# Expert weights in rows of 16 KB, and down into one bank: a transformer pair on one Trainium2 core

## The chip, the cores and the metric

One core of a Trainium2 chip runs the whole program; the other cores have no part in it. The metric is the device time of one execution in microseconds (us). The kernel before took 2298.34 us (median of 3 runs, 2297.22 to 2298.34). A difference of 0.2%, some 4.6 us, is about the least that can be told from no change.

## The reference, cut to what matters

Two blocks follow each other on 256 tokens of width 1024, all in float32. The first block has a modulation from a vector `c` (`w_ada`, 1024 by 6144), projections (`w_in`, 1024 by 3072) with retention and dilated attention, an output product, and a mixture of 16 experts. The second block is two rounds of FFN, gated recurrent mixer, FFN.

```
mod = silu(c) @ w_ada + b_ada                   # six parts of 1024
h = rmsnorm(x, g_pre_mix) * (1 + scale_m) + shift_m
proj = h @ w_in                                 # retention q, k, v, gate; attention q, k, v
x = x + gate_m * rmsnorm(mixed @ w_out, g_post_mix)
h = rmsnorm(x, g_pre_ffn) * (1 + scale_f) + shift_f
affinity = softmax(h @ w_router)                # 256 x 16
gates, idx = top_k(affinity.T, 32)              # each expert takes its 32 best tokens
for e in range(16):
    xe = h[idx[e]]                              # 32 x 1024
    ye = (silu(xe @ w_gate[e]) * (xe @ w_up[e])) @ w_down[e]   # 1024 -> 2048 -> 1024
    out[idx[e]] += ye * gates[e]
x = x + gate_f * rmsnorm(out, g_post_ffn)
```

The three weights of an expert are 8 MiB each, 24 MiB together; 16 experts are 384 MiB, each byte read once.

## The kernel before, in words

The kernel is written in a tile framework: a scheduler orders the instructions of each engine beforehand, by priorities and estimated times, and sets the waits; `s.queue` pins an instruction behind another of its engine. Each engine then works its list in that order. All large loads are issued by SP, in order, and a load waits at the head of SP's list until its buffer is free.

**Units.** `unit` (L53) loads a weight block of 8 KB a partition (1 MiB) into a ring. The first block has two rings, `ring` with RA = 4 and `ringb` with RB = 7 buffers, taken in a fixed mixture: 11 MiB ahead at most. The second block has `ring` alone.

**The front.** `mod_bank` (L226) forms part i of the modulation by products with 32 equal columns, a unit being two tiles of 128 rows; the later parts are summed on VectorE, a unit at a time (`mod_unit`, L278, called by `mod_step`). The projections take `w_in` in units of 256 columns, so that a row of a unit is 1 KB (`unit(c)`, L383). `pieces` (L253) splits them in high and low parts on ScalarE, VectorE and GpSimd; `chan` (L385) makes one tile of 128 channels from a unit. Sixteen such tiles follow each other (L574), and between them the modulation and the attention and retention heads. `shift` (L424) reads units 6, 8, 10 and 11 once more.

**Routing.** The affinities are sorted, and one-hot matrices `sall` of token against slot are made. `gather0(k)` (L727) picks the first expert's rows of tile k of the model width, `gathers(k)` (L730) those of all 16 experts, each by four products.

**Experts** (`experts`, L793). For each expert, and each k of 8 tiles of the model width, a unit of gate and one of up: 128 rows of 2048 columns, so that a row of a unit is 8 KB and a partition holds one row. Each unit serves four products of 32 stationary columns against 512 moving ones (L817), the four groups of FFN columns standing in four groups of 32 rows of one PSUM bank. For the first expert `gather0` and `gathers` stand between the units, and the last six of its units that find no place in the ring (`more`, L767) go to tiles that serve no more. Then silu, product, transposes to `ht` (L835), and down: units of two groups of 128 rows of 1024 columns, so that a row is 4 KB; eight products a unit (L855) into two banks `dn`, one for each half of the model width, four row groups in each. `fin` adds the result of an expert to the tokens during the next. The last expert takes down by columns, 512, 256 and 256 (L875), in rows of 2 KB and 1 KB, so that what stands behind the last weights is small: one copy `pr` (L885) of 256 columns, products with the gates (L887), and `rms` (L324).

**Second block.** `boundary` (L958) normalises, and FFN's first units are already being loaded: two units (gate and up half of its first 256 columns) stand in SP's list behind the last expert's.

## Time and profile before

| | us |
|---|---|
| median of three runs | 2298.34 |
| profiled execution, its span | 2296.9 |
| what lies around the span (median less span) | 1.4 |
| front, until the first product of an expert | 192.6 |
| experts, until the last weights of down are used | 192.6 to 1133.1 |
| second block, from its first FFN product | 1148.9 to 2296.9 |

The page gives one profiled execution. Its first part is busy time by engine; its second cuts the span in 40 slices of 57.4 us and shows the share of each engine in tenths, the granted clock of TensorE, the share of the 16 DMA engines and the GB/s that they moved. The chain is followed back from the last instruction to whatever released each step. PE is TensorE, PEld its weight loads, DVE VectorE, ACT ScalarE, POOL GpSimd, SP the queue that issues loads. A float32 product is shown as two instructions.

### The profile page before, as it was taken

What the parts mean: (1) busy time and instruction counts of PE and PEld (TensorE: products, weight loads), DVE (VectorE), ACT (ScalarE), POOL (GpSimd) and SP (SyncE); (2) the same over time, 40 slices, a digit from 0 to 9 for tenths busy, and PEclk for the clock granted to TensorE, in tenths of its full rate; (3) what the DMA queues carried; (4) which work ended last, traced back from release to release, by engine and by line L of the source; (5) the groups of instructions that cost most, each with busy time, mean ns of one, the idle gap of its engine ahead of it and who ended that gap; (6) DMA issues with size and microseconds to landing.
All of it is one profiled execution on the core that took longest, in us unless ns stands there. A gap on an engine that the chain in (4) does not pass through costs nothing.

```text
span 2296.9 us, 30296 instructions
## 1 busy us (share of the span) xinstructions
PE 1989.6 (87%) x12509; PEld 1334.1 (58%) x12509; DVE 987.9 (43%) x1582; ACT 739.2 (32%) x1224; POOL 155.8 (7%) x164
## 2 busy tenths in 40 slices
PE   7898877777777776767599999999999999999998
PEld 5684211111111111111199999899999998989997
DVE  7984100000000010000275568965556556896554
ACT  4552000000000000000154456845445444684443
POOL 1321000000000000000100032200000003200000
PEclk8997887777888788888799999999999999999999
DMA  8978999999999999999975545546556564544651
GB/s 307 367 292 310 413 417 417 416 417 417 416 417 417 418 417 417 417 417 417 342 247 190 196 158 183 175 149 236 183 174 205 181 207 152 192 165 160 226 180 60
DMA packets 258264, 659.64 MB, mean 287 GB/s; under 512 B 12371, under 2 KB 166219, under 8 KB 225742
## 3 DMA queue, kind: packets, MB, share of 16 engines
q1 hardware_dynamic: 256396, 657.08, 75.9%
q8 instruction: 98, 1.61, 0.3%
q10 hardware_dynamic: 1730, 0.64, 0.1%
q14 instruction: 40, 0.33, 0.0%
HBM read 656.62 MB, written 1.05 MB: 286 GB/s over the span
## 4 chain that ended last, share of the span: by engine, by line
PE 51%; DMA 38%; DVE 4%; POOL 2%; ACT 1%; issue 1%; POOLq 0%; SPq 0%; DVEq 0%; ACTq 0%
DMA w<-in_w_up_e_dram 22%; DMA w<-in_w_down_e_dram 12%; PE up L96 8%; PE up L98 8%; PE up L97 8%; PE acc L98 6%; PE acc L97 6%; PE acc L96 6%; PE up L131 3%; DMA w<-in_w_gate_e_dram 3%; PE up L135 2%; PE acc L817 2%; POOL uc L1187 1%; DVE macc L286 1%; DVE v L1218 1%
## 5 line engine op out<-in xcount | busy, mean ns | idle before, releaser
L83 DVE TENSOR_TENSOR hl<-w,hl 128x1024 fp32r<-128x1024 f32 x376 | 457.5, 1229 | 253.8 <-ACT hl L82 253.8
L82 ACT ACTIVATE hl<-w 128x1024 fp32r<-128x1024 f32 x388 | 404.8, 1057 | 271.1 <-PE up L98 105.3
L96 PE MATMUL up<-hTh,hl 128*128 128x256 f32 x1664 | 470.1, 283 | 1.2 <-ACT uc L1208 1.2
L97 PE MATMUL up<-hTl,hl 128*128 128x256 f32 x1664 | 467.4, 281 | 0.0
L98 PE MATMUL up<-hTh,hl 128*128 128x256 f32 x1664 | 467.4, 281 | 0.0
L96 PEld LDWEIGHTS up<-hTh,hl 128*128 128x128 f32 x1664 | 313.3, 188 | 4.0 <-ACT uc L1208 1.9
L97 PEld LDWEIGHTS up<-hTl,hl 128*128 128x128 f32 x1664 | 313.6, 188 | 2.0
L98 PEld LDWEIGHTS up<-hTh,hl 128*128 128x128 f32 x1664 | 313.5, 188 | 0.0
L855 PE MATMUL up<-w,tmp 128*32 128x512 f32 (+1 forms) x1048 | 222.0, 629 | 55.9 <-DMA w<-in_w_down_e_dram 51.5
L832 DVE TENSOR_TENSOR tmp<-tmp,acc 128x512 f32<-128x512 f32 x16 | 11.0, 687 | 498.8 <-PE acc L817 498.8
L96 PE MATMUL acc<-hl,a 128*128 128x512 f32 x528 | 209.9, 397 | 0.0
L97 PE MATMUL acc<-hl,a 128*128 128x512 f32 x528 | 208.6, 395 | 0.0
L98 PE MATMUL acc<-hl,e 128*128 128x512 f32 x528 | 208.5, 395 | 0.0
L821 ACT ACTIVATE tmp<-acc 128x512 f32<-128x512 f32 x16 | 9.6, 597 | 580.8 <-PE acc L817 580.8
L855 PEld LDWEIGHTS up<-w,tmp 128*32 128x32 f32 x1048 | 48.9, 114 | 217.7 <-DMA w<-in_w_down_e_dram 130.9
L817 PE MATMUL acc<-w,rqk 128*32 128x512 f32 x480 | 97.1, 896 | 51.8 <-DMA w<-in_w_up_e_dram 26.3
L817 PE MATMUL acc<-w,ak 128*32 128x512 f32 x480 | 92.5, 860 | 56.9 <-DMA w<-in_w_gate_e_dram 30.0
L817 PE MATMUL acc<-w,rv 128*32 128x512 f32 x480 | 97.3, 898 | 49.9 <-DMA w<-in_w_gate_e_dram 25.0
L147 POOL TENSOR_TENSOR y<-v,mhalf 128x1 f32<-128x1 f32 x22 | 12.2, 554 | 1827.8 <-DVE v L143 1819.9
L871 DVE COPY pr<-up 128x512 f32<-128x512 f32 x15 | 10.4, 692 | 248.5 <-PE up L855 248.5
L98 PEld LDWEIGHTS acc<-hl,e 128*128 128x128 f32 x528 | 99.0, 187 | 24.3 <-DVE e L916 0.2
L96 PEld LDWEIGHTS acc<-hl,a 128*128 128x128 f32 x528 | 99.1, 188 | 21.4
(371 smaller groups left out, 2364.6 us busy)
## 6 DMA issues: line engine op xcount, KB each, us to landing
w<-in_w_gate_e_dram SPq DMA_DIRECT2D x126, 1024.0 KB, 19.8
w<-in_w_up_e_dram SPq DMA_DIRECT2D x125, 1024.0 KB, 19.8
w<-in_w_down_e_dram SPq DMA_DIRECT2D x123, 1024.0 KB, 17.9
w<-in_ffn_w_up_dram SPq DMA_DIRECT2D x88, 1024.0 KB, 5.3
w<-in_w_in_dram SPq DMA_DIRECT2D x52, 1024.0 KB, 6.6
w<-in_ffn_w_down_dram SPq DMA_DIRECT2D x44, 1024.0 KB, 5.7
w<-in_w_ada_dram SPq DMA_DIRECT2D x24, 1024.0 KB, 9.0
w<-in_w_out_dram SPq DMA_DIRECT2D x12, 1024.0 KB
```

What stands on the lines that cost most here:

```text
L82: a = s.nc.scalar.activation(t[:, 0], src, AF.Copy)
L83: b = (eng or s.nc.vector).tensor_tensor(t[:, 1], src, t[:, 0].bitcast(F32), OP.subtract)
L96: a = mm(out, st[0], mv[0], start=start, stop=False)
L97: mm(out, st[0], mv[1], start=False, stop=False)
L98: s.mm = mm(out, st[1], mv[0], start=False, stop=stop)
L131: a = mm(out, h[0][:, k, tok(t)], ws[k // 4][i][:, k % 4, :], start=k + i == 0, stop=False)
L135: s.mm = mm(out, h[1][:, k, tok(t)], ws[k // 4][0][:, k % 4, :], start=False, stop=k == KT - 1)
L286: s.nc.vector.scalar_tensor_tensor(acc, w[:, a, :], c, acc, OP.mult, OP.add)
L817: T.matmul(gu[i][32 * g:32 * g + 32, :], xk, u[g], start=k == 0, stop=k == KT - 1)
L855: T.matmul(dn[n][32 * g:32 * g + 32, c], ht[:, j, 32 * g:32 * g + 32], u(g), start=j == 0, stop=j == 3)
L1187: G.tensor_tensor(nx[:, lo:], cur[:, lo:], cur[:, lo - sh:16 + S - sh], OP.add)
L1218: V.scalar_tensor_tensor(v, c[:, 13 + k:13 + k + S], self.cw[:, k, hd:hd + 1], v, OP.mult, OP.add)
```

## The change

- **Blocks** (`block`, new): 2 MiB, 16 KB a partition. Two blocks of three go to `ringb` (now 4 buffers of 16 KB) by one load, each third goes to two buffers of `ring` by two loads of 8 KB rows at a pitch of 16 KB. So 12 MiB ahead at most, six blocks. All large weights of the first block go through `block`.
- **Gate and up**: a block is 256 rows of the weight, partition p holding rows 2p and 2p + 1 one behind the other: 16 KB in a row. To match, the tiles of the model width are woven: tile k of x, of the one-hot gathers, of the router weights and of the two factors `af` and `bf` takes every second channel of a group of 256 (`pairs`; `fcol` has the bias and gain columns in that order).
- **Down**: a block is 512 rows, partition p holding rows 4p to 4p + 3: 16 KB in a row. The transposes of h take every fourth column (`hj`). The eight products of a row set go to one bank `dn`: half n of the width in rows 64n to 64n + 63, odd and even j in the two groups of 32 of it. One copy `pr` of 512 columns follows instead of two, and the products with the gates take 64 rows for each half.
- **Last expert**: down is taken as for the others; the three column parts are gone.
- **First expert**: `gathers` of all eight tiles stand behind the transposes of h, ahead of the gates' transposes and of down, and no longer between the units. Four `gather0` stand ahead of the first product, not two. The last 6 MiB of its first weights go to the same idle tiles as before, as three blocks.
- **Projections**: `w_in` in blocks of 512 columns (rows of 2 KB), each used by four tiles; the attention values take 512 moving columns in two banks. `w_ada` comes as blocks of four tiles of 128 rows, `w_out` likewise.
- A reserve for dynamic DMA descriptors is made smaller in the constructor; comments are dropped.

```diff
-RA, RB = 4, 7
+RA, RB = 4, 4
...
-        r = s.ring
-        if s.ringb is not None and s.nunit * RB % (RA + RB) < RB:
-            r = s.ringb
         if t is None:
-            s.nunit += 1
-            t = r.tile([P, 2048], F32, tag="w", name="w")
+            t = s.ring.tile([P, 2048], F32, tag="w", name="w")
...
+    def block(s, view):
+        s.nblock += 1
+        sh = view.shape
+        if s.nblock % 3 == 0:
+            h = sh[1] // 2
+            return [s.unit(view[:, i * h:(i + 1) * h]) for i in range(2)]
+        t = s.ringb.tile([P, 4096], F32, tag="w", name="w")
+        if len(sh) == 3:
+            t = t.rearrange("p (a b) -> p a b", a=sh[1])
+        s.udma = s.nc.sync.dma_start(t, view)
+        h = sh[1] // 2
+        return [t[:, :h], t[:, h:]]
...
+    def ada(s, I, i, u):
+        return s.block(I["w_ada"][0, u * 512:(u + 1) * 512, i * D:(i + 1) * D].rearrange("(a p) n -> p a n", p=P))
     def mod_bank(s, I, i):
         pt = s.bank("up")
-        for u in range(4):
-            w = s.unit(I["w_ada"][0, u * 256:(u + 1) * 256, i * D:(i + 1) * D].rearrange("(a p) n -> p a n", p=P))
-            for a in range(2):
+        for u in range(2):
+            w = s.ada(I, i, u)
+            for a in range(4):
                 for n in range(2):
-                    r = 32 * (2 * a + n)
-                    s.nc.tensor.matmul(pt[r:r + 32, :], s.cb[:, 2 * u + a, :], w[:, a, half(n)], start=u == 0, stop=u == 3)
+                    r = 32 * (2 * (a % 2) + n)
+                    k = 4 * u + a
+                    s.nc.tensor.matmul(pt[r:r + 32, :], s.cb[:, k, :], w[a // 2][:, a % 2, half(n)], start=k < 2, stop=k > 5)
...
-    def mod_unit(s, I, i, u, acc, first):
-        w = s.unit(I["w_ada"][0, u * 256:(u + 1) * 256, i * D:(i + 1) * D].rearrange("(a p) n -> p a n", p=P))
+    def mod_unit(s, w, u, acc, first):
...
+    def pairs(s, ap, k):
+        return ap.rearrange("p (q c r) -> p q r c", r=2, c=P)[:, k // 2, k % 2, :]
...
+        wide = lambda c: s.block(wv[:, :, c * 512:(c + 1) * 512])
+        us = {}
+        def chan(c, j, n):
             pt = s.bank("up")[:, :n]
-            for q, w in enumerate(s.pieces(u[:, :, tok(j)])):
+            if c // 2 not in us:
+                us[c // 2] = wide(c // 2)
+            o = (c % 2) * S + j * P
+            for q in range(2):
+                w, = s.pieces(us[c // 2][q][:, :, o:o + P])
...
-        us = {c: unit(c) for c in (10, 11, 6, 8)}
-        for q, c in enumerate((10, 11)):
-            pt = s.bank("up", (2, S))
-            ws = s.pieces(us[c])
-            for t in range(2):
-                for k in range(KT):
-                    w = ws[k // 2]
-                    s.mm3(pt[:, t, :], (h[0][:, k, tok(t)], h[1][:, k, tok(t)]), (w[0][:, k % 2, :], w[1][:, k % 2, :]), k == 0, k == KT - 1)
-            A.activation(av[:, :, q * S:(q + 1) * S], pt, AF.Copy)
+        us = {c: wide(c) for c in (5, 3, 4)}
+        pts = [s.bank("up") for t in range(2)]
+        for q in range(2):
+            for i, w in enumerate(s.pieces(us[5][q])):
+                k = 4 * q + i
+                for t in range(2):
+                    s.mm3(pts[t], (h[0][:, k, tok(t)], h[1][:, k, tok(t)]), (w[0][:, 0, :], w[1][:, 0, :]), k == 0, k == KT - 1)
+        for t in range(2):
+            A.activation(av[:, t, :], pts[t], AF.Copy)
...
-            s.mod_unit(I, j, u, accm[j], j > 2)
+            if u % 2 == 0:
+                accm["w"] = s.ada(I, j, u // 2)
+            s.mod_unit(accm["w"][u % 2], u, accm[j], j > 2)
...
-        wu = {c: wo(c) for c in (2, 3, 0, 1)}
+        wu = {}
+        for c in (1, 0):
+            wu[2 * c], wu[2 * c + 1] = s.block(I["w_out"][0, c * 512:(c + 1) * 512, :].rearrange("(j p) n -> p j n", p=P))
...
-                T.matmul(pt, xh[:, t, tok(k)], sl, start=t == 0, stop=False)
-                T.matmul(pt, xl[:, t, tok(k)], sl, start=False, stop=t == 1)
+                T.matmul(pt, s.pairs(xh[:, t, :], k), sl, start=t == 0, stop=False)
+                T.matmul(pt, s.pairs(xl[:, t, :], k), sl, start=False, stop=t == 1)
...
-        more = [extra((pe, "dk", 2048, 1)), extra((pe, "yg", 2048, 1)), extra(wt, wt), extra(wt, wt),
-                extra((pa, "ya", 1024, 1), xt), extra(xt, tt, tt)]
+        more = [extra((pe, "dk", 2048, 1), (pe, "yg", 2048, 1)), extra(wt, wt, wt, wt),
+                extra((pa, "ya", 1024, 1), xt, xt, tt, tt)]
...
+        def load(w, e, r, x=None):
+            v = I[w][0, e, r[0]:r[1], :].rearrange("(p r) f -> p (r f)", p=P)
+            if x:
+                return x(v)
+            return [u[:, g * 512:(g + 1) * 512] for u in s.block(v) for g in range(4)]
...
+            for q in range(4):
                 if e == 0:
-                    for i in range(k + (k > 0), min(k + 2, KT)):
-                        gather0(i)
-                    if k:
-                        gathers(k - 1)
-                xk = xe[k // 2][:, k % 2, ec] if e else x0[:, k, :]
+                    for k in range(2 * q + (q > 0) * 2, min(2 * q + 4, KT)):
+                        gather0(k)
                 for i, w in enumerate(("w_gate_e", "w_up_e")):
-                    n = 2 * k + i - RA - RB
-                    v = I[w][0, e, tok(k), :]
-                    if e == 0 and n >= 0:
-                        u = more[n](v)
-                    else:
-                        u = s.unit(v)
-                        u = [u[:, g * 512:(g + 1) * 512] for g in range(4)]
-                    for g in range(4):
-                        T.matmul(gu[i][32 * g:32 * g + 32, :], xk, u[g], start=k == 0, stop=k == KT - 1)
-            if e == 0:
-                gathers(KT - 1)
+                    u = load(w, e, (256 * q, 256 * q + 256), more[i] if e == 0 and q == 3 else None)
+                    for r in range(2):
+                        k = 2 * q + r
+                        xk = xe[k // 2][:, k % 2, ec] if e else x0[:, k, :]
+                        for g in range(4):
+                            T.matmul(gu[i][32 * g:32 * g + 32, :], xk, u[4 * r + g], start=k == 0, stop=k == KT - 1)
...
+            hj = h.rearrange("p (c j) -> p j c", j=4)
             for j in range(4):
-                T.transpose(pt[:, j, :], h[:, tok(j)], s.ident)
+                T.transpose(pt[:, j, :], hj[:, j, :], s.ident)
             ht = s.tmp().rearrange("p (j c) -> p j c", j=4)
             A.activation(ht, pt, AF.Copy)
+            if e == 0:
+                for k in range(KT):
+                    gathers(k)
...
+                for t in range(2):
+                    for n in range(2):
+                        T.matmul(py[t][n], s.ident, ye[t][:, half(n)], start=True, stop=False)
...
-            dn = [s.bank("up") for _ in range(2)]
-            wd = I["w_down_e"][0, e].rearrange("(g j p) n -> p j g n", g=4, p=P)
-            def down(n, j, u, c=slice(0, 512)):
-                for g in range(4):
-                    T.matmul(dn[n][32 * g:32 * g + 32, c], ht[:, j, 32 * g:32 * g + 32], u(g), start=j == 0, stop=j == 3)
-            pr = pa.tile([P, D], F32, tag="xn", name="pr", bufs=2)
-            if e < NE - 1:
+            dn = s.bank("up")
+            for g in range(4):
+                u = load("w_down_e", e, (512 * g, 512 * g + 512), more[2] if e + g == 0 else None)
                 for j in range(4):
-                    us = []
-                    for q in range(2):
-                        v = wd[:, j, 2 * q:2 * q + 2, :]
-                        if e + j + q == 0:
-                            us += more[-1](v)
-                        else:
-                            u = s.unit(v)
-                            us += [u[:, a, half(n)] for a in range(2) for n in range(2)]
                     for n in range(2):
-                        down(n, j, lambda g: us[2 * g + n])
-                A.activation(pr[:, half(0)], dn[0], AF.Copy)
-                V.tensor_copy(pr[:, half(1)], dn[1])
-            else:
+                        r = 64 * n + 32 * (j % 2)
+                        T.matmul(dn[r:r + 32, :], ht[:, j, 32 * g:32 * g + 32], u[2 * j + n], start=g == 0 and j < 2, stop=g == 3 and j > 1)
+            pr = pa.tile([P, 512], F32, tag="xn", name="pr", bufs=2)
+            V.tensor_copy(pr, dn)
+            if e == NE - 1:
                 res = [([], py[t]) for t in range(2)]
-                for n, c in ((0, slice(0, 512)), (1, slice(0, 256)), (1, slice(256, 512))):
-                    w = c.stop - c.start
-                    o = slice(n * 512 + c.start, n * 512 + c.stop)
-                    m = 512 // w
-                    for t in range(2):
-                        T.matmul(py[t][n][:, c], s.ident, ye[t][:, o], start=True, stop=False)
-                    for j in range(0, 4, m):
-                        u = s.unit(wd[:, j:j + m, :, o])
-                        for i in range(m):
-                            down(n, j + i, lambda g: u[:, i, g, :], c)
-                    V.tensor_copy(pr[:, o], dn[n][:, c])
-                    for t in range(2):
-                        T.matmul(py[t][n][:, c], gT[:, tok(t)], pr[:, o], start=False, stop=True)
-                        res[t][0].append((py[t][n][:, c], o))
+                for t in range(2):
+                    for n in range(2):
+                        r = slice(64 * n, 64 * n + 64)
+                        T.matmul(py[t][n], gT[r, tok(t)], pr[r, :], start=False, stop=True)
+                        res[t][0].append((py[t][n], half(n)))
             def fin(t, e=e, gT=gT, pr=pr):
                 for n in range(2):
                     pt = s.bank("tr")
-                    T.matmul(pt, gT[:, tok(t)], pr[:, half(n)], start=True, stop=True)
+                    r = slice(64 * n, 64 * n + 64)
...
+                    T.matmul(pt, gT[r, tok(t)], pr[r, :], start=True, stop=True)
```

## Rows read from the trace of the kernel before

**Rows 1.** The page: DMA share and GB/s in 40 slices, and the packets

```profile
DMA  8978999999999999999975545546556564544651
GB/s 307 367 292 310 413 417 417 416 417 417 416 417 417 418 417 417 417 417 417 342 247 190 196 158 183 175 149 236 183 174 205 181 207 152 192 165 160 226 180 60
DMA packets 258264, 659.64 MB, mean 287 GB/s; under 512 B 12371, under 2 KB 166219, under 8 KB 225742
```

**Rows 2.** The chain in order of time: start us, us, what

```profile
242.43 19.85 DMA w<-in_w_up_e_dram
...
324.13 18.80 DMA w<-in_w_down_e_dram
...
1048.38 18.47 DMA w<-in_w_down_e_dram
```

**Rows 3.** Windows: PE, PEld, DVE, ACT, POOL busy, clock, DMA share, GB/s; two experts, whole stage

```profile
324.00:340.00 16.00, 11.85 (x58) 2.90 (x54) 1.05 (x3) 0.87 (x2) 0.00 (x0) 1.00 1.03 409
344.00:380.00 36.00, 23.91 (x126) 3.69 (x120) 3.45 (x5) 0.60 (x1) 0.00 (x0) 0.83 1.01 421
1048.00:1064.00 16.00, 11.82 (x58) 2.73 (x54) 1.05 (x3) 1.47 (x3) 0.00 (x0) 0.92 1.03 409
1068.00:1104.00 36.00, 27.76 (x128) 4.65 (x124) 3.44 (x5) 0.60 (x1) 0.00 (x0) 0.78 1.02 422
264.00:1108.00 844.00, 614.40 (x2898) 117.47 (x2894) 71.35 (x146) 31.24 (x59) 0.00 (x0) 0.82 1.02 417
```

**Rows 4.** Windows: the last expert's down, the first expert's down, the front

```profile
1108.00:1133.00 25.00, 17.84 (x118) 6.45 (x118) 3.33 (x7) 2.71 (x7) 0.00 (x0) 0.86 1.02 347
224.00:232.00 8.00, 7.09 (x66) 2.96 (x70) 1.02 (x5) 0.87 (x2) 0.00 (x0) 1.00 0.58 223
100.00:148.00 48.00, 47.55 (x369) 44.17 (x370) 45.15 (x84) 25.26 (x64) 8.42 (x7) 0.95 0.91 341
```

**Rows 5.** Timeline of the front: start, us, engine, line, op, count, idle before

```profile
18.03 1.06 PE L235 MATMUL up<-w,cb 128*32 128x512 f32 x8 [1.52 <-DMA w<-in_w_ada_dram]
53.96 0.37 SPq L69 DMA_DIRECT2D w<-in_w_in_dram  x1
64.80 1.93 PE L430 MATMUL tr<-w,shb 128*32 128x256 f32 x32
68.87 1.14 PE L457 MATMUL acc<-ak,aq 64*128 64x256 f32 x8
```

**Rows 6.** Timeline: the first expert's beginning

```profile
190.39 0.36 PE L723 MATMUL tr<-sall,xhh 128*128 128x32 f32 x1 [0.37 <-DVE sall L714]
192.55 3.64 PE L817 MATMUL acc<-w,x 128*32 128x512 f32 x16
194.55 10.16 SPq L69 DMA_DIRECT2D w<-in_w_down_e_dram  x5
197.00 0.77 PE L723 MATMUL acc<-sall,xhh 128*128 128x512 f32 x1
```

**Rows 7.** Timeline: the last expert and the way into the second block

```profile
1094.31 1.93 PE L817 MATMUL acc<-w,rqk 128*32 128x512 f32 x8 [0.55 <-DMA w<-in_w_up_e_dram]
1109.23 1.06 PE L817 MATMUL acc<-w,rv 128*32 128x512 f32 x8
1122.09 0.69 DVE L885 COPY pr<-up 128x512 f32<-128x512 f32 x1 [10.97 <-PE up L855]
1124.62 5.68 SPq L69 DMA_DIRECT2D w<-in_ffn_w_up_dram  x2
1133.06 0.64 PE L855 MATMUL up<-w,tmp 128*32 128x256 f32 x8 [0.76 <-DMA w<-in_w_down_e_dram]
1136.58 0.54 POOL L147 TENSOR_TENSOR y<-v,mhalf 128x1 f32<-128x1 f32 x1 [943.55 <-DVE v L143]
1138.06 1.41 DVE L785 SCALAR_TENSOR_TENSOR x<-acc,yx,x 128x512 f32<-128x512 f32 x2
1148.94 1.43 PE L131 MATMUL up<-hl,hTh 128*128 128x256 f32 x5
```

More of the change, by code (lines that the diff above doesn't have):

```diff
@@ L191, in cols @@
             r += v.shape[0]
+        res["all"] = c
         return res
@@ L291, in mod_sum_cols @@
         for k in range(KT):
-            s.nc.tensor.matmul(pt[:, k, :], acc[:, tok(k)], s.one[:, :2], start=True, stop=True)
-        mc = s.sm.tile([P, KT], F32, tag="mc", name="mc", bufs=4)
-        s.nc.vector.tensor_tensor(mc, s.bada[:, 8 * i:8 * i + 8], pt[:, :, 0], OP.add)
-        return mc
+            s.nc.tensor.matmul(pt[:, k, :], s.pairs(acc, k), s.one[:, :2], start=True, stop=True)
+        mc = s.sm.tile([P, 4, 2], F32, tag="mc", name="mc", bufs=4)
+        s.nc.vector.tensor_tensor(mc, s.fcol[:, 4 + 4 * i:8 + 4 * i, :], pt.rearrange("p (q r) o -> p q r o", r=2)[:, :, :, 0], OP.add)
+        return mc
+    def pairs(s, ap, k):
+        return ap.rearrange("p (q c r) -> p q r c", r=2, c=P)[:, k // 2, k % 2, :]
     def mod_sum_rows(s, acc, out):
@@ L357, in first @@
         V.memset(one, 1.0)
+        pt = s.bank("tr", (2, 28))
+        v = c0["all"][:, 16:72].rearrange("p (k h) -> p h k", h=2)
+        even = s.ident.rearrange("p (c r) -> p r c", r=2)
+        for hf in range(2):
+            for r in range(2):
+                T.matmul(pt[64 * hf:64 * hf + 64, r, :], even[:, r, :], v[:, hf, :], start=True, stop=True)
+        fcol = sm.tile([P, 2, 28], F32, name="fcol", bufs=1)
+        V.tensor_copy(fcol, pt)
+        s.fcol = fcol.rearrange("p r k -> p k r")
         xn = [s.norm_rows(t, x) for t in range(2)]
@@ L429, in shift @@
                     r = 32 * (2 * (k % 2) + n)
-                    T.matmul(pt[r:r + 32, :], shb[:, k, :], us[c[n]][:, k, :], start=k < 2, stop=k > 5)
+                    o = (c[n] % 2) * S
+                    T.matmul(pt[r:r + 32, :], shb[:, k, :], us[c[n] // 2][k // 4][:, k % 4, o:o + S], start=k < 2, stop=k > 5)
             m = s.tmp()[:, :S]
@@ L574, in first @@
         for n, c in enumerate((7, 9, 0, 1, 2, 3, 4, 5)):
-            u = unit(c)
             for j in range(2):
                 i = 2 * n + j
-                pt = chan(u, j, NH)
+                pt = chan(c, j, NH)
                 sca = 0.125 if c == 1 else 1.0
@@ L606, in first @@
         A.activation(ex, rg[:, 3, :1], AF.Exp)
-        wo = lambda c: s.unit(I["w_out"][0, c * S:(c + 1) * S, :].rearrange("(j p) n -> p j n", p=P))
-        wu = {c: wo(c) for c in (2, 3, 0, 1)}
+        wu = {}
+        for c in (1, 0):
+            wu[2 * c], wu[2 * c + 1] = s.block(I["w_out"][0, c * 512:(c + 1) * 512, :].rearrange("(j p) n -> p j n", p=P))
         y = [pd.tile([P, KT * NH], F32R, tag=n, name="y" + n)[:, :KT * S].rearrange("p (k n) -> p k n", k=KT) for n in ("hh", "hl")]
@@ L659, in logits @@
                 for j in range(4):
-                    T.transpose(pt[:, j, :], x[:, t, tok(4 * hf + j)], s.ident)
+                    T.transpose(pt[:, j, :], s.pairs(x[:, t, :], 4 * hf + j), s.ident)
                 if hf:
```

21 lines of the change are left out of this document (8 added, 13 removed).

## The prediction

> **What bounds the kernel now.** I read the slices of the page first. They show three kernels in one: a front of four slices with loads at 290 to 370 GB/s, then fifteen slices with the DMA engines full and an even 417 GB/s, then twenty slices in which loads run at half that [rows 1]. The chain says what the middle is: one load behind the other, two for each third of an expert, hardly an instruction between them [rows 2]. From the load at 324.13 to that at 1048.38 lie 12 experts, so an expert takes 60.35 us for 24 MiB. TensorE is busy 614 of 844 us there, ScalarE and VectorE far less [rows 3]: the stage is bound by the rate of the loads, and whatever the engines do within it is hidden. In the front TensorE is busy 47.6 of 48 us [rows 4]: it is bound by computing. The second block, untouched, starts when the mixture is done; it counts only as a shift.
>
> So the question is what sets 417 GB/s. Cutting the stage by what is being loaded gives the answer. While down arrives (rows of 4 KB) the rate is 409 GB/s, while gate and up arrive (rows of 8 KB) 421 or 422; the rows are the first and the last of 13 such pairs, which run from 408 to 411 and from 420 to 422 [rows 3]. The last expert's down, in rows of 2 and 1 KB, comes at 347 [rows 4]. The rate depends on the length of a row. On the page 258264 packets less 225742 leave 32522 of 8 KB or more, about the 254 units of gate and up times 128 rows: a row of 8 KB is one packet [rows 1].
>
> **Steady stage: the large term.** Means of the pairs, 409.8 and 420.7 GB/s, are 2.559 and 2.492 us a MiB. A MiB is 16 rows of 4 KB on each of 16 engines, or 8 rows of 8 KB; 8 rows fewer saved 0.066 us, so a row costs 8.3 ns beside its bytes. (Check: 16 x 2.492 + 8 x 2.559 = 60.35 us, the measured period.) Rows of 16 KB save 4 more a MiB: 2.459 us, 426 GB/s. After the change an expert has 16 MiB in 16 KB rows and 8 MiB in 8 KB rows: 16 x 2.459 + 8 x 2.492 = 59.29 us, 1.06 less. From the second expert's last up to the last expert's are 14 periods: **-14.8 us**. No row of 16 KB is in this trace. The bounds: the 8 KB rate may be a ceiling, then only down gains, 24 x 2.492 = 59.82, -7.4 us; the extremes of the windows, 408 and 422, would make a row 10.6 ns, and 14 x 128 rows of it -19 us. I take the straight line through the two rates, as the pair is so even.
>
> [...]
>
> **Can the engines and SP follow?** [...] The count of products does not change. The loads ahead are 12 MiB instead of 11, freed six blocks behind. The halved work of `pr`, the strided transposes and `fin` on 64 rows lie beside loads; without that cover `fin` would cost up to 1.7 us an expert either way.
>
> **Last down.** Before: from the last up (1109.23) to the last weights (1133.06) 23.8 us [rows 7]. After: 6 x 2.459 + 2 x 2.492 = 19.7 us: **-4.1** (-3.9 at the 8 KB rate).
>
> **Behind the last weights.** Before, little is exposed: 1133.06 to the addition at 1138.06, 5.0 us [rows 7]. After: 16 instructions of the last block 2.1 us, copy of 512 columns 0.69, a pair of gate products. Their halves stand on 64 rows each; four such products of 256 columns took 1.14 us in the front [rows 5], so the pair of 512 takes 1.1. Two squares of 512 columns 1.3 to 1.5, power 0.54, small steps 0.8, gaps 0.4: 7.1 us, +2.1. [...] TensorE stands between those levels here, 0.86 [rows 4]: **+3.0**. FFN's first two units are issued at 1124.62 before [rows 7]; after, their slots in the ring have long been free, and they queue right behind the last block, landing some 6 us after it (1 KB rows), ahead of the 10.9 us that the second block needs to its first product (1138.06 to 1148.94).
>
> **Front.** The modulation of part 1 ends on 2 MiB blocks: 16 instructions instead of 8 behind the last landing, 1.06 us [rows 5]: **+1.05**. The attention values' products are half as many and twice as wide: no change in columns. Then SP's queue. The block of values (the third) keeps its buffers until `shift` has read it, about 66.7 [rows 5]; the ninth block, `w_ada`, waits for them, and behind it on SP stand all others: the first new `w_in` block, whose buffer is also freed then. Before, SP resumed at 53.96 [rows 5]. So the ninth block lands at about 74, the tenth near 80. The steps of part 2 that read the ninth are due from about 70, the tile that reads the tenth is the fifth of sixteen: due near 85 at 5.1 us a tile (64.8 to the mixer at 147). VectorE may wait some us for the ninth. Nothing or 8 us (the whole delay of the ninth and tenth): I take **+1.5**, near the lower end, as other work stands between. Blocks eleven to twenty come at 5.1 us each, faster than the tiles want them. Rows of 2 KB instead of 1 KB in `w_in` shorten loads that are hidden: nothing.
>
> **Restart at the first expert.** The ring is full when routing ends, and SP's first issue follows the first products (194.55) [rows 6]. The second expert's last up lands at 262.28 [rows 2]: 67.7 us for 23.5 MiB (16.5 had been issued: 11 units, 5 more of gate and up, half a unit of down), which want 59.1; 8.6 are lost, 3.7 of them while down is waited for (224 to 232, 223 GB/s) [rows 4]. After: 12 + 4 + 1.5 MiB are there, 22.5 remain, 55.6 us. The other 4.9 lost, from issue to data and at the last landing above all, I leave. Two more `gather0` stand ahead, eight products of 0.36 and their way out, about 1.6 [rows 6]. [...] Together 9.5, so 65.1: **-2.6** (+2 to -6).
>
> **Sum.** +1.05 + 1.5 - 2.6 - 14.8 - 4.1 + 3.0 = -15.95 us. The profiled span of 2296.9 becomes 2280.95; the median of the runs lies 1.4 above the span: **2282.4 us**.
>
> **Rivals.**
> *8 KB is the ceiling*, by itself or because a row of 16 KB is sent in parts. For it: no row here is longer, and 421 may be what the memory gives. Against: 409 to 421 shows no bend. Steady -7.4, last down -3.9, restart 0.7 less: -7.65, **2290.7 us**.
> [...]
> *Slower: the front starves.* Blocks of 2 MiB in six places, half of them held for four tiles: if SP's in-order queue turns the three wide `w_in` blocks into a chain of free, issue, land (5 us of loading and 2.5 of latency), each costs 7.5 us on an engine that is busy throughout. One such stall leaves 2289.9, three give -15.95 + 22.5 = +6.55: **2304.9 us**; from just over two on the gain is gone. For it: SP waits at the head of its list, and VectorE and TensorE have no slack in the front. Against: only the first wide block is released close to its need.
>
> **Chances.** Forecast 0.62 (its own range 2273 to 2288), ceiling 0.18, dear end 0.12, starved front 0.08. One run can tell 0.2%, 4.6 us, from no change: faster means under 2293.7. All but the starved front and a sum of two rivals lie there: faster 0.85, same 0.07, slower 0.08. The low end takes the -19 us bound and the better end of the restart (2274.8) with some room, the high end both middle rivals: 2270 to 2293.5.
>
> **What would show it.** Windows of gate, up and down alike near 424 to 426 GB/s, and a period near 59.3 us; 421 throughout would be the ceiling. Packets of 8 KB and more as many as before, but those of 4 KB gone. The last up to the last weights in under 20 us, then 7 to 8 us to the addition. First product of an expert at 194 to 198; later than 205 means the front starves. A period above 60 us would make all of it wrong.

## The result, and the profile after

The changed kernel takes 2282.37 us (median of 4 runs, 2279.80 to 2283.66) against 2297.78 (4 runs) of the kernel before: ratio 0.9930, 95% interval 0.9919 to 0.9942. The forecast was 2282.4. Runs of one kernel spread by 1 to 7 us, so single microseconds below are read from traces, not from medians. A trace is one execution, and two of them can differ by 2 us in one stage.

The page of the changed kernel, its rows as in [rows 1] (DMA share and GB/s in 40 slices of the span, then the packets):

```profile
DMA  8878999999999999999875645546546554544651
GB/s 334 322 296 323 425 424 425 426 425 425 422 424 424 426 426 425 426 424 426 308 246 175 204 162 185 176 161 222 183 159 222 178 201 165 177 170 164 221 185 56
DMA packets 212821, 659.60 MB, mean 289 GB/s; under 512 B 9555, under 2 KB 147019, under 8 KB 180174
```

The same bytes go in 45443 packets fewer. Packets of 8 KB and more are 212821 less 180174, 32647, about as many as before (32522); those from 2 to under 8 KB (225742 less 166219, 180174 less 147019) fell from 59523 to 33155. In the fifteen full slices 417 GB/s became 422 to 426. The second block's slices are much as they were.

The chain of the changed kernel (start us, us, what), to be held against [rows 2]:

```profile
243.35 17.77 DMA w<-in_w_up_e_dram
...
314.34 26.06 DMA w<-in_w_down_e_dram
...
1085.27 27.73 DMA w<-in_w_down_e_dram
```

The first is the second expert's last up, landing at 261.12; the others are the last block of down of the third and of the last expert, at 340.40 and 1113.00: 772.60 us for 13 experts, 59.43 a period, where [rows 2] gives 60.35 (60.50 by the table below, over 14 periods).

TensorE's timeline of the changed kernel at the joints of the stages, answering to [rows 6, 7]:

```profile
196.47 1.92 PE L853 MATMUL acc<-w,x 128*32 128x512 f32 x2
...
261.16 3.64 PE L853 MATMUL acc<-w,rv 128*32 128x512 f32 x16 [3.83 <-DMA w<-in_w_up_e_dram]
...
1093.22 3.03 PE L853 MATMUL acc<-w,rv 128*32 128x512 f32 x16 [0.45 <-DMA w<-in_w_up_e_dram]
...
1113.04 3.36 PE L899 MATMUL up<-w,tmp 128*32 128x512 f32 x16 [1.39 <-DMA w<-in_w_down_e_dram]
1117.31 1.99 PE L907 MATMUL acc<-pr,gT 64*128 64x512 f32 x8 [0.92 <-DVE hb L1169]
1130.67 1.94 PE L972 MATMUL tr<-ident,xn 128*128 128x128 f32 x8 [11.38 <-DVE xn L960]
1132.45 2.07 PE L141 MATMUL up<-hl,hTh 128*128 128x256 f32 x8
```

These cut the span at the same events in both kernels: the first expert's first product, the second expert's last up (landing 262.28 before, 261.12 after), the last expert's last up, its last weights, the second block's first product (1148.94 before), the end.

| stretch | before | after | measured | predicted |
|---|---|---|---|---|
| start to first product | 192.55 | 196.47 | +3.92 | +2.55 |
| to the second expert's last up | 69.73 | 64.65 | -5.08 | -2.6 |
| 14 periods | 846.95 | 832.10 | -14.85 | -14.8 |
| last up to last weights | 23.83 | 19.82 | -4.01 | -4.1 |
| last weights to the second block | 15.88 | 19.41 | +3.53 | +3.0 |
| second block | 1147.96 | 1148.05 | +0.09 | 0 |
| span | 2296.90 | 2280.50 | -16.40 | -15.95 |

The two large terms came within 0.1 us. Front and restart were off by 1.4 and 2.5 us to opposite sides, so that the total fits better than its parts.

### The profile page after: what moved, and what is told of

The parts are those of the page before. It is cut to its first block, busy times and chain, and to the rows that moved or that the text cites. A ratio compares the mean times of both kernels' runs of the same rounds, so it can differ in the third digit from the quotient of the medians.

```text
span 2280.5 us, 29819 instructions
## 1 busy us (share of the span) xinstructions
PE 1887.8 (83%) x12429; PEld 1324.4 (58%) x12429; DVE 985.6 (43%) x1577; ACT 730.1 (32%) x1205; POOL 158.6 (7%) x164
## 2 busy tenths in 40 slices
DMA packets 212821, 659.60 MB, mean 289 GB/s; under 512 B 9555, under 2 KB 147019, under 8 KB 180174
## 4 chain that ended last, share of the span: by engine, by line
PE 56%; DMA 34%; DVE 5%; ACT 2%; POOL 2%; issue 1%; ACTq 0%; POOLq 0%; DVEq 0%; SPq 0%
DMA w<-in_w_down_e_dram 17%; DMA w<-in_w_up_e_dram 12%; PE up L106 8%; PE up L108 8%; PE up L107 8%; PE acc L107 6%; PE acc L108 6%; PE acc L106 5%; DMA w<-in_w_gate_e_dram 4%; PE up L141 3%; PE acc L853 3%; PE up L899 3%; PE up L145 2%; POOL uc L1208 1%; DVE v L1239 1%
## 5 line engine op out<-in xcount | busy, mean ns | idle before, releaser
L899 PE MATMUL up<-w,tmp 128*32 128x512 f32 x1008 | 166.0, 792 | 91.4 <-DMA w<-in_w_down_e_dram 87.2
L899 PEld LDWEIGHTS up<-w,tmp 128*32 128x32 f32 x1008 | 31.8, 132 | 207.9 <-DMA w<-in_w_down_e_dram 138.5
L853 PE MATMUL acc<-w,rqk 128*32 128x512 f32 x480 | 89.3, 883 | 74.5 <-DMA w<-in_w_gate_e_dram 51.2
L853 PE MATMUL acc<-w,rv 128*32 128x512 f32 x480 | 85.5, 823 | 72.7 <-DMA w<-in_w_up_e_dram 53.5
L106 PEld LDWEIGHTS acc<-hl,a 128*128 128x128 f32 x528 | 99.2, 188 | 21.4
L107 PEld LDWEIGHTS acc<-hl,a 128*128 128x128 f32 x528 | 99.1, 188 | 21.4
```

Source lines behind the costliest of these rows:

```text
L106: a = mm(out, st[0], mv[0], start=start, stop=False)
L107: mm(out, st[0], mv[1], start=False, stop=False)
L853: T.matmul(gu[i][32 * g:32 * g + 32, :], xk, u[4 * r + g], start=k == 0, stop=k == KT - 1)
L899: T.matmul(dn[r:r + 32, :], ht[:, j, 32 * g:32 * g + 32], u[2 * j + n], start=g == 0 and j < 2, stop=g == 3 and j > 1)
```

## The experiments

**The price of a row, by itself** (m1). A kernel of loads only, nine stretches:

```
PHASES = [(4096, 4096, 16), (2048, 4096, 16), (1024, 4096, 16), ...]   # row elements, elements a partition, loads
v = src[o:o + P * m].rearrange("(r p f) -> p r f", p=P, f=row)
nc.sync.dma_start(t.rearrange("p (r f) -> p r f", f=row), v)
```

> Loads alone, nothing computed: 32 MiB of expert weights in each of nine stretches, as 2 MiB loads with rows of 16, 8, 4, 2 and 1 KB, then 1 MiB loads with 8 KB rows, 0.5 MiB loads with 4 KB rows, 4 MiB loads with 32 KB rows, and 2 MiB with 16 KB again. Theory (each row costs 8.3 ns of a DMA engine beside its bytes, 2.426 us a MiB): 426, 421, 410, 390 and 355 GB/s for 16 to 1 KB, 429 for 32 KB, and the size of a load changes nothing: 421 for 8 KB and 410 for 4 KB rows in small loads too. Rival, a ceiling at 8 KB: 421 for 8, 16 and 32 KB. Rival, the size of a load sets the rate: 2 MiB loads of 8 and 4 KB rows as fast as those of 16 KB, and 1 and 0.5 MiB loads slower.

One run; its windows, one inside each stretch (stretch, length, POOL busy, clock, DMA share, GB/s):

```profile
8.00:80.00 72.00, 0.00 (x0) 1.00 1.01 429
88.00:160.00 72.00, 0.00 (x0) 1.00 1.01 422
168.00:240.00 72.00, 0.00 (x0) 1.00 1.03 410
250.00:324.00 74.00, 0.00 (x0) 1.00 1.05 387
336.00:420.00 84.00, 0.00 (x0) 1.00 1.10 348
436.00:500.00 64.00, 0.00 (x0) 1.00 1.01 422
512.00:580.00 68.00, 0.00 (x0) 1.00 1.03 410
592.00:656.00 64.00, 0.00 (x0) 1.00 1.00 432
664.00:740.00 76.00, 0.00 (x0) 1.00 1.00 427
```

16, 8, 4, 2 and 1 KB rows: 429, 422, 410, 387, 348. The same 422 and 410 come in loads of 1 and 0.5 MiB: the size of a load changed nothing. 32 KB rows give 432, 16 KB again 427. As us a MiB (1048576 bytes by the rate, 428 for 16 KB) that is 3.013, 2.709, 2.558, 2.485, 2.450, 2.427 for 64, 32, 16, 8, 4 and 2 rows on each engine: 9.5, 9.5, 9.1, 8.7 and 11 ns a row from step to step (the last two come from differences of 4 to 6 GB/s, so they are rough). One straight line from 1 to 32 KB, no ceiling at 8; the price is nearer 9.4 ns than the predicted 8.3. Rows of 1 KB lose a fifth against 16 KB here (348 against 429).

**The rows taken back, all else kept** (e1).

```
-            v = I[w][0, e, r[0]:r[1], :].rearrange("(p r) f -> p (r f)", p=P)
...
+            v = I[w][0, e, r[0]:r[1], :].rearrange("(r p) f -> p r f", p=P)
...
```

> The changed kernel with the same loads of 2 MiB (and 1 MiB for every third block), the same buffers and order, but a partition's piece of a load taken as rows half as long: gate and up in rows of 8 KB, down in rows of 4 KB, as the kernel before had them. (The weights' rows then don't meet the woven channels, so the output is another; the instructions are the same.) Theory (a price per row): the period of an expert goes back to 16 x 2.492 + 8 x 2.559 = 60.35 us, 14 periods give back 14.8 us, the last down 0.8, the restart about 1: 2299 us. Rival (the gain came from fewer and larger loads, or from 12 MiB instead of 11 ahead): period 59.3, 2282 us.

2299.38 us (10 runs, before 2298.70; ratio 1.0004, 0.9995 to 1.0013): the whole gain is gone, with the same number of loads, the same buffers and the same 12 MiB ahead (only the three first blocks that go to idle tiles kept their rows). Last up of the second and of the last expert:

```profile
262.35 3.18 PE L854 MATMUL acc<-w,rv 128*32 128x512 f32 x16 [3.91 <-DMA w<-in_w_up_e_dram]
...
1110.88 2.84 PE L854 MATMUL acc<-w,rv 128*32 128x512 f32 x16 [0.28 <-DMA w<-in_w_up_e_dram]
```

848.53 us in 14 periods, 60.61 each against 59.43 by the same rows of the changed kernel: 1.18 for 128 rows on each engine, 9.2 ns a row. The rival (larger and fewer loads, more look-ahead) falls.

**The rows lengthened further** (e2). Each third block still came in halves with 8 KB rows, because its buffers are the second block's 8 KB ones. Here the first block has a pool of its own of two 16 KB buffers at the same place.

```
-        if s.nblock % 3 == 0:
-            return [s.unit(view[:, i * h:(i + 1) * h]) for i in range(2)]
-        t = s.ringb.tile([P, 4096], F32, tag="w", name="w")
+        t = (s.ringb if s.nblock % 3 else s.ringa).tile([P, 4096], F32, tag="w", name="w")
...
+            s.ringa = c1.enter_context(tc.tile_pool(name="ringa", bufs=RA // 2))
```

> The changed kernel with every block, the third ones too, as one load in 16 KB rows, in 6 buffers of 16 KB (before 4 of 16 and 4 of 8, the same memory). Theory (a price per row): the period falls to 24 x 2.459 = 59.02 us, 14 times 0.27 = 3.7 us less, with the first and the last expert 4.1: 2278.3 us. Rival (the memory gives no more than the 424 GB/s of the mix, or the 1 MiB pieces were worth something as they come free early): no change, 2282 to 2284 us.

2275.34 us (4 runs, 2273.80 to 2276.72; ratio 0.9903, 0.9889 to 0.9916). Its page and joints:

```profile
GB/s 335 338 288 320 428 428 427 428 427 428 425 428 427 427 428 428 428 428 427 312 228 199 198 152 181 194 157 209 198 146 223 188 197 163 177 175 162 220 186 56
DMA packets 203652, 659.59 MB, mean 290 GB/s; under 512 B 8451, under 2 KB 145915, under 8 KB 179070
```

```profile
194.16 1.92 PE L849 MATMUL acc<-w,x 128*32 128x512 f32 x2
...
260.19 2.82 PE L849 MATMUL acc<-w,rv 128*32 128x512 f32 x16 [2.97 <-DMA w<-in_w_up_e_dram]
...
1086.81 3.41 PE L849 MATMUL acc<-w,rv 128*32 128x512 f32 x16 [1.11 <-DMA w<-in_w_up_e_dram]
...
1106.52 1.92 PE L895 MATMUL up<-w,tmp 128*32 128x512 f32 x16 [1.80 <-DMA w<-in_w_down_e_dram]
```

The period is 826.62 / 14 = 59.04, 0.39 less: 5.4 of the 8.5 us that the span lost. 0.27 was expected, and m1's rates for 8 and 16 KB give 0.28; what the other 0.1 us a period is, no run shows. The rest is not of rows: the front came 2.3 sooner (below), the restart is 1.3 longer, and in this execution TensorE took 1.92 instead of 3.36 us for the last 16 instructions.

**The end behind the last weights** (e3, e5). First the very last block in two loads:

```
+        for o in (0, h) if last else (None,):
+            a = t if o is None else t[:, o:o + h]
+            s.udma = s.nc.sync.dma_start(a, view if o is None else view[:, o:o + h])
```

> The changed kernel with the very last block of expert weights in two loads of 1 MiB into the same buffer. Theory (what stands behind the last landing is on the path: 16 instructions in 3.36 us at the half clock): 8 remain, 1.7 us less, less 0.1 for the rows: 2280.8 us. Rival (the end behind the last weights is set by the clock and by ScalarE's and GpSimd's steps, or by the second block's first loads): no change, 2282.4 us.

2281.01 us (5 runs, 2280.00 to 2281.39). The median fits; but 1.4 us less than another median is within the spread, and in the trace the shorter end (gate products 21.79 behind the last up, 24.09 in the changed kernel) stands behind a front that came 1.8 later. Not settled by the time alone. The other traces settle it: where the 16 instructions of the unsplit block took 1.92 us, the gate products start 22.5 to 22.6 behind the last up (e2, e4, e6, e8, e9), with the split 21.7 to 21.8 (e3, e10, e11). So the split is worth 0.8 to 0.9 us, and the other 1.5 of the 2.3 come with the clock: 3.36 against 1.92 us, at a granted 0.50 in the changed kernel and 1.00 in e8 (1108 to 1116).

Then down in two banks again:

```
-            dn = s.bank("up")
+            dn = [s.bank("up") for _ in range(2)]
...
-                        r = slice(64 * n, 64 * n + 64)
-                        T.matmul(py[t][n], gT[r, tok(t)], pr[r, :], start=False, stop=True)
+                        T.matmul(py[t][n], gT[:, tok(t)], pr[:, half(n)], start=False, stop=True)
```

> The changed kernel with down in two banks again: the 32 products of an expert as before, each four groups of 32 rows deep in a bank for each half of the columns, two copies (ScalarE and VectorE) and gate products over 128 rows. Theory (within the stage all of it lies beside loads, and behind the last weights the two copies run side by side): no change, 2282.4 us, plus or minus 1. Rival (one bank saves a copy and half the depth of the gate products on the path, 14 times or at the end): 2 us or more slower, 2284.5 us.

2283.58 us (5 runs, 2281.85 to 2285.53), between the two. Last weights and gate products:

```profile
1113.22 3.67 PE L899 MATMUL up<-w,tmp 128*32 128x512 f32 x16 [1.90 <-DMA w<-in_w_down_e_dram]
1117.65 6.11 PE L907 MATMUL acc<-pr,gT 128*128 128x512 f32 x8 [0.77 <-ACT pr L901]
```

The eight gate products took 1.99 us in the changed kernel, on 64 rows each and at a granted clock of 0.93 (1116 to 1124); here it is 0.59, so these rows don't tell depth from clock. The stage does, where `fin` has the same products, at a granted clock of 1.00: six instructions on 128 rows take 3.03 us in the kernel before (at 344.82, two banks there too), four on 64 rows 1.13 in the changed kernel (at 1060.31). By that estimate the four ahead of the first squares take 2.0 us on 128 rows, 0.9 more than on 64. The periods are equal ((1093.45 - 261.31) / 14 = 59.44). So one bank is worth nothing within the stage and about 1 us at the end; the medians, 1.2 us apart, can't tell.

**The gathers back between the quarters** (e6).

```
+                    for k in range(2 * q - 2, 2 * q) if q else ():
+                        gathers(k)
```

> The changed kernel with the gathers of the other experts back between the quarters of the first one, two of eight behind each. Theory (they take 7.6 us of TensorE; ahead of down they delay nothing, since the six blocks that gate and up have freed feed the DMA queue to 231 and down's first products come at 226): no change, 2282.4 us, plus or minus 1. [...]

2283.83 us (5 runs, 2279.90 to 2284.72). From first product to the second expert's last up it takes 264.17 - 198.10 = 66.07 us, the changed kernel 64.69: nothing is won back, so no stall stood here to be removed. The windows of the changed kernel say the same, beside [rows 4]:

```profile
224.00:232.00 8.00, 8.00 (x58) 3.34 (x61) 3.45 (x8) 0.38 (x1) 0.00 (x0) 1.00 1.02 431
...
196.00:204.00 8.00, 8.00 (x33) 2.72 (x35) 0.65 (x3) 0.00 (x0) 0.10 (x1) 0.50 0.22 58
```

The DMA engines are full at 224 to 232 (223 GB/s before); from 196 to 204 they are nearly empty, while SP waits for the first buffers.

**VectorE's order in the front** (e4, e8). VectorE's and TensorE's rows of the changed kernel where the modulation's first part ends:

```profile
20.86 1.29 DVE L285 TENSOR_TENSOR hl<-w,hl 128x512 fp32r<-128x512 f32 x2 [4.78 <-ACT hl L282]
22.07 0.68 DVE L253 COPY tmp<-up 128x512 f32<-128x512 f32 x1
```

```profile
22.81 0.66 PE L262 MATMUL tr<-ident,tmp 128*128 128x128 f32 x4 [3.38 <-DVE tmp L253]
```

Its products ended at 19.4, but the copy stands behind two subtractions that wait for the third block. The program has the copy first; the order comes from the framework's planning. What turned it round is not shown: with the third block in one load (e2) the copy stands first again (19.09), but so it does with that block in two loads of 1 MiB, each of half the columns (e9, 19.35). In the kernel before the transposes start at 19.91. A first try moved one subtraction:

```
+            if s.lead and eng is s.nc.vector:
+                s.queue(b, s.lead)
+                s.lead = None
...
+        s.lead = V.scalar_tensor_tensor(am, sc_m, 1.0, c0["g_pre_mix"], OP.add, OP.mult)
```

> The changed kernel with one order written out: the first subtraction of the split of w_in on VectorE is issued behind the step that makes the scale am, as it stood in the kernel before; nothing else. In the changed kernel two such subtractions stand ahead of the copy of the modulation, wait 4.78 us for the third block to land (20.86 to 22.07), and the transposes behind that copy start at 22.81 with 3.38 us of waiting where the kernel before has 0.81. Theory (2.6 of the 3.9 us that the front lost are this place in VectorE's queue): the first product of an expert comes 2.5 to 2.9 us sooner, near 193.7, 2279.7 us. Rival (the front's end is set by the blocks that land late for the modulation's other parts, or VectorE, busy throughout from 72 to 108, swallows the gain): no change, 2282.4 us.

2281.60 us (5 runs, 2279.78 to 2282.77): a miss, since the edit didn't do what it was for. The second subtraction took the first one's place:

```profile
21.61 0.69 DVE L285 TENSOR_TENSOR hl<-w,hl 128x512 fp32r<-128x512 f32 x1 [5.51 <-ACT hl L282]
22.22 0.68 DVE L253 COPY tmp<-up 128x512 f32<-128x512 f32 x1
```

There is a second such place. The last steps of the modulation's part 5 come late and delay the retention's normalisation, whose power (POOL) TensorE awaits; here VectorE, then POOL, of the changed kernel, then the power of the kernel before:

```profile
145.77 1.25 DVE L301 SCALAR_TENSOR_TENSOR av<-w,sc,av 128x1024 f32<-128x1024 f32 x1
...
147.61 1.27 DVE L301 SCALAR_TENSOR_TENSOR av<-w,sc,av 128x1024 f32<-128x1024 f32 x1
148.80 0.72 DVE L569 TENSOR_SCALAR v<-mv 128x4 f32<-128x4 f32 x1
```

```profile
150.68 1.01 POOL L570 TENSOR_TENSOR y<-v,mhalf 128x4 f32<-128x4 f32 x1
```

```profile
146.36 1.02 POOL L535 TENSOR_TENSOR y<-v,mhalf 128x4 f32<-128x4 f32 x1 [5.98 <-DVE v L534]
```

These steps wait for no load: from 68 to 148 no wait of VectorE is on DMA, and it is busy for 77.2 of the 80 us.

So both orders were written out: all subtractions of that block behind `am`, and the last four steps behind the normalisation (each step is one instruction of 1.27 us).

```
+            if s.lead and eng is s.nc.vector:
+                s.queue(b, s.lead)
...
+        for u in (2, 3):
+            s.mod_unit(accm["w"][u % 2], u, accm[5], True, s.rn)
```

> The changed kernel with two places of VectorE's order written out. First: all subtractions of the split of the first w_in block stand behind the step that makes am (the run before this one had moved one of them only, and another took its place ahead of the copy: 21.61, with 5.51 us of waiting). Second: the last four accumulation steps of modulation part 5 (1.27 us each, at 141.83 to 147.61 in the changed kernel, ended at 141.6 in the kernel before) stand behind the retention's normalisation, which they had pushed from 146.12 to 148.80. Theory (these two orders are 2.6 and 2.4 of the 3.9 us that the front lost): first product of an expert near 191.5, 2277.4 us. Rival (the late steps only move into the output projection, where VectorE is as scarce): first product near 193.9, 2279.8 us. Rival (noise of the granted clock in the front): 2282.4 us.

2278.85 us (5 runs, 2276.08 to 2282.60; the profiled run was the fastest). Rows of TensorE, VectorE and ScalarE (the last, here called the mixture's squares, is the sum of squares for the norm of `mixed @ w_out`):

```profile
19.96 0.66 PE L262 MATMUL tr<-ident,tmp 128*128 128x128 f32 x4 [0.81 <-DVE tmp L253]
...
191.95 1.92 PE L861 MATMUL acc<-w,x 128*32 128x512 f32 x2
```

```profile
144.96 1.27 DVE L303 SCALAR_TENSOR_TENSOR av<-w,sc,av 128x1024 f32<-128x1024 f32 x1
...
152.62 1.27 DVE L303 SCALAR_TENSOR_TENSOR av<-w,sc,av 128x1024 f32<-128x1024 f32 x1
```

```profile
167.28 0.70 ACT tmp L352 x2
```

The first product is at 191.95, near the 191.5 expected, but not as theory had it. With the first order in place the sixteenth projection tile, whose bias column ScalarE takes at 142.07 here, is far sooner than in the changed kernel, 5.8 us instead of the 2.6 expected. ScalarE's rows at the thirteenth tile, at the sixteenth and at the squares, first of the changed kernel, then the thirteenth tile of e8, then the last two of the kernel before:

```profile
134.15 0.17 ACT L617 ACTIVATE bcol<-up 128x1 f32<-128x1 f32 x1 [0.81 <-PE up L108]
...
147.87 0.17 ACT L617 ACTIVATE bcol<-up 128x1 f32<-128x1 f32 x1 [0.82 <-PE up L108]
...
172.00 0.70 ACT tmp L348 x2
```

```profile
128.35 0.17 ACT L623 ACTIVATE bcol<-up 128x1 f32<-128x1 f32 x1 [0.55 <-PE up L108]
```

```profile
147.17 0.17 ACT L581 ACTIVATE bcol<-up 128x1 f32<-128x1 f32 x1 [0.82 <-PE up L98]
...
168.86 0.70 ACT tmp L329 x2
```

The two orders were not run apart in this form, but at the thirteenth tile the 5.8 us are already there (128.35 against 134.15), and the four steps that the second order moves stood at 138.27 and later in the changed kernel. So the second order has no part in them. Behind the sixteenth tile it brought nothing: from that tile to the squares it takes 25.2 us (24.1 in the changed kernel, 21.7 before). The steps, now at 144.96 to 152.62, only stand in the output projection's way, as the first rival had it.

**The front's loads as before** (e9).

```
-        wide = lambda c: s.block(wv[:, :, c * 512:(c + 1) * 512])
+        wide = lambda c: s.block2([wv[:, :, i * S:(i + 1) * S] for i in (2 * c, 2 * c + 1)])
...
-            return [s.unit(view[:, i * h:(i + 1) * h]) for i in range(2)]
+            return s.block2([view[:, i * h:(i + 1) * h] for i in range(2)])   # a 3-d view: two loads
```

> The changed kernel, its experts untouched, with the front's loads as before: modulation, w_in and w_out in units of 1 MiB (w_in 256 columns wide in 1 KB rows), two of them in the halves of each 16 KB buffer, and the values of the attention column half by column half. Theory (2 MiB blocks land later and the order of VectorE's steps turns out worse for it): the front goes back to the 192.55 of the kernel before plus 0.9 for the two gathers ahead of the first product, 193.5, so 3 us less: 2279.4 us. Rival (the loss comes with the woven rows and with buffers held in pairs, not with the width of the loads): 2282.4 us.

2279.39 us (4 runs, 2277.85 to 2280.03), 3 less than the changed kernel, as expected; but in the traces only 1.9 of it is the front's (first product at 194.54 against 196.47, 193.5 expected), and 1.4 is the clock at the end (granted 0.93 from 1108 to 1116, 0.50 in the changed kernel), where the last 16 products took 1.92 us instead of 3.36. The first product and the power:

```profile
194.54 1.92 PE L865 MATMUL acc<-w,x 128*32 128x512 f32 x2
```

```profile
147.28 1.02 POOL L582 TENSOR_TENSOR y<-v,mhalf 128x4 f32<-128x4 f32 x1 [6.03 <-DVE v L581]
```

The sixteenth tile is no sooner (147.72), though the copy at 19 us stands first again. But the power is back from 150.68 to 147.28, and from that tile to the squares it takes 22.1 instead of 24.1 us. This is beyond the spread: the five kernels whose front is the changed one's (the changed kernel, e1, e3, e5, e6) all take 24.1 there. Their first products, from 196.35 to 198.28, differ by as much as the 1.9 us. Buffers are still held in pairs and rows still woven, so the 2 us came with the width of the loads, or with the values' products, which went back with it.

**Together** (e7, e10, e11). e7 is e2 with e3's split and e4's order; e10 is e2 with e3's split and both orders of e8; e11 is e2 with e3's split and e9's front.

> All blocks in 16 KB rows in 6 buffers, with the last block of the last expert in two loads and the order on VectorE in the front written out. Theory: all blocks in 16 KB rows alone were 2275.3 us; there the order on VectorE had already come out right and the first product stood at 194.2, so the order gives nothing more, the split of the last block 0.9 (8 instructions fewer at the full clock) to 1.7 (at the half clock): 2274 us. Rival (the terms of end and front are noise between runs): 2275.3 us or more.

2275.28 us (4 runs, 2270.63 to 2277.18): the rival's number; split and order add nothing that the medians can tell.

> All blocks in 16 KB rows in 6 buffers, both orders on VectorE written out, the last block of the last expert in two loads. Theory: all blocks in 16 KB rows were 2275.3 us with the first order already right; the second order gives up to 2.4, the split nothing measurable so far: 2273 us. Rival (VectorE has no room for the late steps in the output projection either): 2275.3 us.

2278.99 us (4 runs, 2276.70 to 2280.31): worse. The late steps end at 158.5, and from the sixteenth tile (145.65) to the squares it takes 27.8 us.

> The two changes that gave something, together: all blocks of the experts in 16 KB rows in 6 buffers, and the front's loads as in the kernel before (1 MiB units, w_in 256 columns wide), two in each 16 KB buffer; the last block of the last expert in two loads. Theory: from the first product on as with all blocks in 16 KB rows (2077.8 us from there to the end of the span, 2077.5 with the last block split), the front as in the run before this (194.5): a span of 2272.1, 2273.9 us. Rival (the gains of the front are the same ones, since all blocks in 16 KB had the right order on VectorE by itself and stood at 194.2): 2275.3 us.

2273.99 us (4 runs, 2273.40 to 2274.22), ratio 0.9892 (0.9875 to 0.9908): as worked out, and the lowest median of all. It is 8.4 us below the changed kernel; against e2's 2275.34 the ranges meet, so the front's part in it is not shown by time.

## Why the prediction was right, point by point

*Steady stage.* Right in mechanism and size: the rate follows the length of a row (348 to 432 GB/s from 1 to 32 KB in m1), 14 periods gave 14.85 us. e1 took it away by the rows alone, m1 showed the line without any computing. The price of a row is 8.3 ns by the change's own difference (1.06 us for 128 rows), 9.2 to 9.5 by e1 and m1. The first rival, a ceiling at 8 KB, is refuted by m1 (422 at 8, 427 to 432 above) and e2. The engines followed: the 16 instructions of a block took 3.64 us at a granted clock of 0.50 (at 1108.01 in the changed kernel), against 4.9 us of loading.

*Last down.* Right, -4.01: the same price, and no rows of 1 and 2 KB any more.

*Behind the last weights.* The size was near, and the clock's share was the chance of one execution: six of the seven other traces with an unsplit last block have the last 16 instructions in 1.92 us. The +3.0 of the sum was set between its 7.1 us and the same end at a lower clock throughout, an estimate that no run shows. What the trace showed in its place: to the addition, which starts at 1121.92, it took 8.9 us (8.0 predicted); the 16 instructions took 3.36 us for 2.1, at a granted clock of 0.50 (1112 to 1116), while copy, gate products and power lasted as their rows said. That is past the 7 to 8 us named as a sign. The second block's first loads were there in time, and the dear end of the chances (0.12) did not come.

*Restart.* The mechanism was half wrong. -5.1 instead of -2.6: the six freed blocks were issued between 201 and 215 and kept the DMA engines full (share 1.01, 426 GB/s from 215 to 230) until the seventh was issued at 230.39; from the first issue at 201.26, six blocks at 4.9 us reach 231. The sum of 9.5 us holds 3 for a DMA queue that is empty while `gathers` stand ahead of down; no run shows them, and with the gathers back between the quarters nothing was won (e6). The extra first gathers stand ahead of the first product, so the table has them in the front; they cost 0.8 us, not 1.6. SP's issue of the ninth block (for the next paragraph) and of the seventh freed one:

```profile
52.55 1.23 SPq L65 DMA_DIRECT2D w<-in_w_ada_dram  x2
...
230.39 1.19 SPq L65 DMA_DIRECT2D w<-in_w_up_e_dram  x2
```

*Front.* The sum's sign was right, the cause wrong. SP did not hold the ninth block until `shift`: it issued it at 52.55, ahead of `shift`'s first product (57.55), so here a buffer was taken as it came free, not in strict turn. Nor did the first tile come later: it is 3.2 us sooner than before (67.86 against 71.07, by ScalarE's bias columns). What cost was behind it: 3.9 us more from the first to the sixteenth tile (80.0 against 76.1), 2.4 from there to the mixture's squares (24.1 against 21.7), and 0.8 to the first product, the gathers; together the +3.92. Of the 3.9 no run shows the cause; it is no wait for a load, as from 68 to 148 none of the engines' waits is on DMA. The 2.4 come with the last modulation steps, which stand later in VectorE's order; e9 takes 2.1 of them back. The wait of 4.78 us at 19 us gave more away: with the right order there the wide loads have the sixteenth tile at 142 to 146 (e2, e7, e8, e10), sooner than the kernel before (147.17). The starved front, the rival on the slower side, did not come: the whole loss is 3.9 us, not 22.5, and no chain of waits for loads. The 2.5 us of latency that this rival takes are near what the page of the kernel before shows: a load of 1 MiB of `w_lru_up` landed 4.8 us after its issue (median of 10), by estimate 2.5 of them for its bytes at 417 GB/s.

*The total.* 2282.4 against 2282.37 rests on the two right terms and on errors that nearly cancel: +1.4 in front, -2.5 at the restart, +0.5 at the end, +0.1 in the second block, and +0.5 from span to median, which lie 1.87 apart where 1.4 was taken. A fit this close was luck.

## What to carry over

Where a stage is nothing but loads, look at the rate by the length of the contiguous run: here a price of 8.7 to 11 ns a row showed as one nearly straight line of us per MiB against rows per MiB (m1), and a reordering of the weights' axes that the neighbours could follow bought 14.85 us in 14 periods without touching the work. Elsewhere wider loads came at a cost: in the front, where the engines are the bound, the order planned for a busy engine was another with them, and the first product stood 3.92 us later. With the copy first again, the wide loads had the first product at 191.3 to 194.2 (e7, e8, e2), the narrow ones at 193.5 and 194.5 (e11, e9), so the width as such cost nothing that these traces can tell (their granted clock from 20 to 60 us differs too, 0.91 in e2 and 0.96 in e7); a poor order cost more (e10, 199.0). So widen loads where DMA is the bound, and elsewhere look first at the order that comes with them. When an order is written out, look whether the next instruction slips into the gap, and what the moved steps will stand in front of.

## What the runs showed of the hardware

One core, with no other at work in the program, drew 432 GB/s in 32 KB rows and 427 to 429 in 16 KB rows, with the DMA share at 1.00 to 1.01; 348 at 1 KB with a share of 1.10 (m1). Prolonged to no rows at all (2.427 less twice 0.0094 us a MiB, both of m1), the line ends at 435 GB/s, an estimate. The size of a load from 0.5 to 2 MiB changed nothing at an equal row length (422 at 8 KB, 410 at 4 KB). TensorE's granted clock differed between executions in the same place: the last 16 products took 3.36 us in the changed kernel's trace and 1.92 in those of e1, e2, e4, e6, e8 and e9, and that alone moves the end by 1.4 us (granted clock from 1108 to 1116: 0.50 in the changed kernel, 1.00 in e8).
